# A hybrid encoder layer on one core: another order of the projection jobs, and linear-attention levels with one instruction per step for both directions

## The chip, the cores and the metric

The kernel runs on one core of one Trainium2 chip. The metric is the device time in microseconds (us) of one execution. Five engines are named as the profile names them: PE is TensorE (matmuls; PEld is its weight load), DVE is VectorE, ACT is ScalarE, POOL is GpSimd, and SP is the engine whose queue issues most of the transfers. Each engine works through its own queue in order and waits on semaphores for the others.

## What is computed

One layer is applied to two request groups with the same parameters: a prompt of 512 tokens and a sample of 1024 tokens, each 1024 wide. The input is normed and modulated, projected by one matrix of 1024 x 3360 whose columns go to four mixers and a gate, and projected back.

```python
def hybrid_layer(x, c, ...):
    shift, scale, gate = split(silu(c) @ ada_w + ada_b, 3)
    h = rms_norm(x, pre_g) * (1 + scale) + shift
    a_q, a_k, a_v, a_lr, b_u, c_q, c_k, c_v, d_u, d_v, z = split(h @ w_in)
    out_a = gla_branch(a_q, a_k, a_v, a_lr, ...)      # gated linear attention, both directions
    out_b = fnet_branch(b_u, fnet_w)                  # real part of a 2-D Fourier transform, then fnet_w
    out_c = attention_branch(c_q, c_k, c_v, ...)      # rms_norm and rotary on q and k; softmax; 8 heads, 2 for k and v
    out_d = sgu_branch(d_u, d_v, ...)                 # u * (w_s @ rms_norm(v) + b_s) in chunks of 128 tokens
    mixed = concat([out_a, out_b, out_c, out_d]) * silu(z)
    return x + gate * rms_norm(mixed @ w_out, post_g)

# gated linear attention of one direction, per head (4 heads, 32 wide in k, 64 in v):
#   a_r = sigmoid(lr_r @ w2 + b2) ** (1 / 16)
#   o_t = sum over s <= t of (q_t * prod(a_r, r = s+1..t)) . k_s  v_s
# the other direction runs over the flipped tokens, with s < t; both are added and normed
```

All inputs and outputs are float32.

## The kernel before

**Groups and jobs.** The 1536 tokens are worked in three groups of 512: group 2 is the prompt, groups 0 and 1 are the halves of the sample. For each group the projection is cut into jobs: A (queries, keys, values and the low-rank gates of linear attention, called GLA), dv and du of the gating mixer with its mix, b (Fourier), kv and q (attention), and z, the gate path, ten jobs of 128 columns. For float32 accuracy every operand is split into a rounded high part and a low part (oph and opl, the halves of a weight tile wt), and each product is three matmuls. A weight unit of 128 x 512 is loaded raw, cast on ACT (L306) and its low part subtracted on POOL (L98), or on DVE where the table LOW_V says so, which it does for job b of group 2; both halves are stored in DRAM (parts), and groups 0 and 1 load them from there (L298). gemm_tm (L314) makes 256 columns for 512 tokens: 8 blocks x 4 token blocks x 3 matmuls of 256 columns. gemm_fm (L337) makes 128 columns with the tokens on the free axis: 8 x 3 matmuls of 512 columns.

**What follows a job.** Nearly all results go to DRAM and come back later. z (L452): three exponential or logarithm passes on ACT (tile ze), one DVE product (zr), a store to zT from SP's queue (L464). q and kv (c_path, L490): an ACT copy (cev, kev), a square, a reduction, an inverse root in small steps, two DVE products, two POOL products (rp_t), one DVE sum, and the store to qd or kvd from SP's queue (L509, L501); this is called rope here (L391). dv and du: ACT copies into dvu; then the mix, twelve matmuls on normed dv and four DVE instructions that read them (L446).

**The main chain.** For group 2: GLA first pass, second pass, Fourier mixer (fnet), key preparation (kv_path), attention. Then GLA of group 0, fnet over groups 0 and 1, GLA of group 1, key preparation and the second GLA pass over both, and the sample's attention in eight stages (attend). The output projections of finished groups (out_first, out_last) run beside it.

**What sets the order.** The jobs are traced inside `later()` (L513), which lowers their priority, so that they fill TensorE beside the main chain. The framework plans the order of each queue when the program is built, from priorities and its own time line. A log, flog, counts the columns of the filler matmuls in thousands; after_columns (L93) queues a matmul behind the point where the log reaches a number. The order of the jobs before: for group 2 and 0, A, dv, du, b, mix, kv, q (jobs, L1220), then z with the input preparation of the next group hooked in before its jobs 6 and 9 (next_prep, L1234), then a part of the gate of the modulation (gate_path). Group 1 starts with b and has its z among the last fillers (L1296).

**GLA first pass (L762).** The two directions are worked as a binary tree with levels m = 1, 2, 4, ..., 64 over 512 tokens. At a level the keys of one half of each pair of m-blocks meet the queries of the other half: qsi and ksx serve one direction, qpi and kpx the other. Each level splits those halves into high and low parts (kh, kl, qh, ql), one instruction for each direction's half, runs 48 matmuls of 32 rows (L815) and puts the result into st under a mask (L820, four DVE copies). Then the queries and keys are multiplied by the products of the decay factors (ntf, ntb). After the levels, st is multiplied with the values (L866, L867, with its casts sth and stl), and the keys are transposed for the states. LEVEL_AT places the level m = 2 of a group, and each later level a step further, in the filler's column count:

```python
LEVEL_AT = {2: (124, 12), 0: (548, 13), 1: (806, 13)}
```

## Time and profile before

| | |
|---|---|
| median of 3 runs | 1240.02 us (1235.35 to 1246.15) |
| the profiled execution | 1240.43 us, span 1238.6 us |
| PE busy | 1105.1 us, 89% of the span |
| DVE, ACT, POOL busy | 61%, 48%, 31% |
| mean granted TensorE clock | 0.943 |
| DMA | 233.99 MB, mean 189 GB/s |

The profile is one execution on the chip. Its page gives busy times, a strip in 40 slices and groups of equal instructions: the line, engine and operation, the tiles as out<-in with shapes, the count, the busy time and the mean in ns, then the idle time of the engine ahead of them and what ended it. Other views group the same records by a stretch of time, by tile, by who waited for whom, or list them in order of time. A line number may be that of a helper, as L86 (all split matmuls), L98 (all subtractions), L101 (products) and L104 (sums).

### The profile page before, as it was taken

Reading aid. Unit: us, or ns where it says so; the run is one execution under the profiler, and the core shown is the slowest. Engines: PE = TensorE matmul, PEld = TensorE weight load, DVE = VectorE, ACT = ScalarE, POOL = GpSimd, SP = SyncE. Lnnn points to the kernel's source line nnn. Section 1 sums busy time; section 2 is a strip of 40 time slices with the busy share of each in tenths; the row PEclk is TensorE's granted clock in tenths of the full one; section 3 lists DMA queues with packets and bytes.
Section 4 is the critical chain, followed back from the end, with each engine's and each line's share of the span. In section 5 each row is a group of like instructions: output and inputs, shape, how many; then the busy total and the mean of one; then the engine's idle time right before and its main releaser. Section 6 shows DMA issues by size and latency. Waiting matters only on the chain. (4 is left out here: it accounts for less than half of the span.)

```text
span 1238.6 us, 21385 instructions
## 1 busy us (share of the span) xinstructions
PE 1105.1 (89%) x7906; PEld 973.3 (79%) x7906; DVE 754.5 (61%) x1440; ACT 597.3 (48%) x1472; POOL 382.0 (31%) x372
## 2 busy tenths in 40 slices
PE   5998779998999888998898899788989999988995
PEld 1587768764999886767898778588989998977995
DVE  6439776647454299552239852774787568686615
ACT  4334246643565235462123244444675667666623
POOL 3136654561011147113016510553141011223003
PEclk9999798998999998999999789789999999999998
DMA  8497656877433765576765346678347333264272
GB/s 316 159 324 243 227 183 202 309 271 234 150 117 116 239 198 159 173 251 199 250 203 168 112 147 194 197 252 282 128 145 247 111 103 94 81 212 130 82 252 97
DMA packets 126393, 233.99 MB, mean 189 GB/s; under 512 B 13092, under 2 KB 65796, under 8 KB 126288
## 3 DMA queue, kind: packets, MB, share of 16 engines
q1 hardware_dynamic: 121624, 227.49, 56.0%
q10 hardware_dynamic: 4664, 5.13, 1.2%
q8 instruction: 62, 1.02, 0.3%
q14 instruction: 43, 0.35, 0.1%
HBM read 162.97 MB, written 69.61 MB: 188 GB/s over the span
## 5 line engine op out<-in xcount | busy, mean ns | idle before, releaser
L86 PE MATMUL ps_mm<-wt,oph 128*128 128x256 f32 x2240 | 443.2, 293 | 20.7 <-DMA wt<-parts 11.0
L86 PEld LDWEIGHTS ps_mm<-wt,oph 128*128 128x128 f32 x2240 | 368.6, 199 | 30.6 <-DMA wt<-parts 11.3
L86 PE MATMUL ps_mm<-wt,opl 128*128 128x256 f32 x1120 | 326.0, 292 | 0.0
L86 PEld LDWEIGHTS ps_mm<-wt,opl 128*128 128x128 f32 x1120 | 222.0, 199 | 1.8
L86 PE MATMUL ps_mm<-oph,wt 128*128 128x512 f32 x576 | 194.8, 410 | 12.7 <-DMA wt<-parts 6.1
L554 DVE TENSOR_REDUCE nm<-ps_s 128x1 f32<-128x512 f32 x160 | 108.9, 686 | 58.6 <-PE ps_s L553 57.8
L86 PEld LDWEIGHTS ps_mm<-oph,wt 128*128 128x128 f32 x576 | 112.8, 197 | 38.9 <-ACT kh L797 3.8
L98 DVE TENSOR_TENSOR ptl<-ps_t,pth 128x512 fp32r<-128x512 f32 x160 | 108.4, 685 | 56.7 <-ACT pth L571 56.2
L98 POOL TENSOR_TENSOR wt<-wr,wt 128x512 fp32r<-128x512 f32 (+1 forms) x68 | 90.4, 1333 | 140.5 <-ACT wt L306 131.9
L571 ACT CAST pth<-ps_t 128x512 fp32r<-128x512 f32 x160 | 91.2, 590 | 65.8 <-PE ps_t L569 64.8
L561 ACT ACTIVATE pr<-ps_s,nm 128x512 f32<-128x512 f32 x160 | 109.5, 692 | 20.9 <-DVE nm L557 16.2
L86 PE MATMUL ps_mm<-opl,wt 128*128 128x512 f32 x288 | 117.9, 409 | 0.0
L569 PE MATMUL ps_t<-cs,pr 128*128 128x128 f32 x640 | 91.6, 276 | 1.1 <-DVE nm L557 0.6
L306 ACT CAST wt<-wr 128x512 fp32r<-128x512 f32 (+1 forms) x80 | 47.6, 597 | 77.5 <-PE ps_mm L86 36.0
L569 PEld LDWEIGHTS ps_t<-cs,pr 128*128 128x128 f32 x640 | 76.3, 143 | 9.5 <-PE ps_s L553 1.0
L101 POOL TENSOR_TENSOR oc<-oc,den 128x256 f32<-128x256 f32 x24 | 14.8, 629 | 220.3 <-DVE oc L104 199.0
L86 PEld LDWEIGHTS ps_mm<-opl,wt 128*128 128x128 f32 x288 | 56.7, 197 | 11.4
L552 PE MATMUL ps_s<-kT,qT 128*128 128x512 f32 x128 | 56.5, 442 | 5.0 <-ACT pr L561 4.8
L98 POOL TENSOR_TENSOR opl<-m,oph 128x512 fp32r<-128x512 f32 x30 | 39.1, 1319 | 52.6 <-ACT oph L1086 52.6
L553 PE MATMUL ps_s<-kT,qT 128*128 128x512 f32 x128 | 51.3, 401 | 0.0
L101 POOL TENSOR_TENSOR yt<-yt,gp 128x512 f32<-128x512 f32 x20 | 25.9, 1293 | 81.9 <-ACT jk L1118 64.8
L86 PE MATMUL ps_o<-pth,vkv 128*128 128x256 f32 x256 | 41.7, 285 | 0.6 <-DVE nm L557 0.6
(349 smaller groups left out, 2112.6 us busy)
## 6 DMA issues: line engine op xcount, KB each, us to landing
wt<-parts SPq DMA_DIRECT2D x136, 512.0 KB, 3.6
parts<-wt SPq DMA_DIRECT2D x68, 512.0 KB, 4.7
wr<-wp SPq DMA_DIRECT2D x48, 256.0 KB, 3.8
adar<-ada SPq DMA_DIRECT2D x16, 512.0 KB, 6.0
zT<-zr SPq DMA_DIRECT2D x30, 256.0 KB, 2.8
zt<-zT SPq DMA_DIRECT2D x30, 256.0 KB, 5.0
mt<-mixd SPq DMA_DIRECT2D x24, 256.0 KB, 5.2
wr<-wo SPq DMA_DIRECT2D x20, 256.0 KB, 4.5
```

The costliest lines, as they stand in the source:

```text
L86: t = T.matmul(out, a, b, start=first and i == 0, stop=last and i == len(terms) - 1, skip_group_check=skip)
L98: e.tensor_tensor(out, a, b, ALU.subtract)
L101: e.tensor_tensor(out, a, b, ALU.mult)
L306: (V.tensor_copy if part_engine(HIGH_V, u, S) is V else S.copy)(h, raw)
L552: T.matmul(sp, qT[:, h, qc], kT[kv][:, kc], start=True, stop=False)
L553: T.matmul(sp, qT[:, h, qc], kT[2 + kv][:, kc], start=False, stop=True)
L554: V.tensor_reduce(nm[:, f:f + 1], sp, AX, ALU.max, negate=True)
L561: S.activation(pr, sps[f], AF.Exp, bias=nm[:, 0:1], accum_out=rsum[:, b, h, f:f + 1])
L569: T.transpose(pt[:, k * 128:(k + 1) * 128], pr[f][:, k * 128:(k + 1) * 128], ident)
L571: S.copy(pth[f][:, :, qc], ptv)
```

## The change

**Order of the jobs.** z follows A at once, in all three groups. dv, du, b and the mix follow, and keys and queries come last (a new function `queries`). Group 1 ends its jobs with kv; its queries take the place that its z had among the last fillers. The input preparation of the next group is cut in two: in_prep_x builds the four diagonal blocks on DVE into one tile, and in_prep_b, behind the kv job, makes one matmul of 512 columns in place of four of 128.

**GLA.** The queries of both directions lie in one tile q2, the keys in k2, the factors in one tile ff of three rows. cross(t, m) is the view that takes the right half of each pair for both directions at once, so each split, each factor product and each level of decay products is one instruction where there were two. An ACT copy fills k2 with the keys twice, and one exponential more fills the third row of ff.

**Places.** LEVEL_AT is changed, and the first fold of fnet is queued behind the end of job b plus 14 thousand columns.

```diff
-HA = 6
-HB = 9
 HC = 3
 LEVELS = (1, 2, 4, 8, 16, 32, 64)
-LEVEL_AT = {2: (124, 12), 0: (548, 13), 1: (806, 13)}
+FOLD_AT = 14
+LEVEL_AT = {2: (131, 12), 0: (571, 12), 1: (829, 12)}
...
+        rsb = gm.tile([128, 512], F32, tag="rsb", bufs=1, name="rsb")
+        for b in range(4):
+            V.tensor_scalar(rsb[:, b * 128:(b + 1) * 128], ident, rs[:, b:b + 1], None, ALU.mult)
+        return rsb
+    def in_prep_b(rsb):
         pt = ps_mm()
-        for b in range(4):
-            dg = gm.tile([128, 512], F32, tag="h32", bufs=3, name="dg")[:, 0:128]
-            V.tensor_scalar(dg, ident, rs[:, b:b + 1], None, ALU.mult)
-            T.matmul(pt[:, b * 128:(b + 1) * 128], ones, dg, start=True, stop=True)
-        rsb = gm.tile([128, 512], F32, tag="rsb", bufs=1, name="rsb")
+        T.matmul(pt, ones, rsb, start=True, stop=True)
         V.tensor_copy(rsb, pt)
...
-    def zpath(g, hooks):
+    def zpath(g):
         job[0] = ("z", g)
         for j in range(10):
-            if j in hooks:
-                hooks[j]()
...
+    def c_kv(g):
...
+    def c_q(g, hook):
+        job[0] = ("c", g)
         for j in range(2):
+            if j:
+                hook()
...
+        ff = pool.tile([128, 3, 512], F32, tag="ff", bufs=1, name="ff")
...
+            f = ff[:, 1 - d, :]
             V.tensor_scalar(f, pl, bg[:, d:d + 1], 0.0, ALU.add, ALU.min)
             sub(G, f, f, t)
+            if d:
+                S.activation(ff[:, 2, :], f, AF.Exp, scale=1.0 / 16.0)
             S.activation(f, f, AF.Exp, scale=1.0 / 16.0)
-            ff.append(f)
...
-        qpi = ppool.tile([128, 512], F32, tag=f"qpi{g}", bufs=1, name=f"qpi{g}")
-        qsi = ppool.tile([128, 512], F32, tag=f"qsi{g}", bufs=1, name=f"qsi{g}")
-        ksx = pool.tile([128, 512], F32, tag="ksx", bufs=1, name="ksx")
-        mul(V, qpi, aq, ff[0])
-        mul(V, qsi, aq, ff[1])
-        prod = pool.tile([128, 512], F32, tag="kpx", bufs=1, name="prod2")
-        for i, src in enumerate((qsi, qpi)):
-            qv, kv, pv = (t.rearrange("p (n two) -> p two n", two=2) for t in (src, ak, prod))
-            mul(G, pv[:, i], qv[:, i], kv[:, 1 - i])
+        pad = 2 * 512 + 2 * LEVELS[-1]
+        q2 = ppool.tile([128, pad], F32, tag=f"q2{g}", bufs=1, name=f"q2{g}")
+        k2 = pool.tile([128, pad], F32, tag="k2", bufs=1, name="k2")
+        qsi, qpi, ksx, kpx = q2[:, 0:512], q2[:, 512:1024], k2[:, 0:512], k2[:, 512:1024]
+        def cross(t, m):
+            v = t[:, 0:2 * (512 + m)].rearrange("p (i c) -> p i c", i=2)[:, :, 0:512]
+            return v.rearrange("p i (n two m) -> p i n two m", two=2, m=m)[:, :, :, 0, :]
+        def pair(t, m):
+            return t.rearrange("p (n two m) -> p two n m", two=2, m=m)
+        mul(V, q2[:, 0:1024].rearrange("p (i c) -> p i c", i=2), aq.unsqueeze(1).to_broadcast([128, 2, 512]), ff[:, 0:2, :])
+        prod = pool.tile([128, 512], F32, tag="prod", bufs=1, name="prod2")
+        for i in range(2):
+            mul(G, pair(prod, 1)[:, i], cross(q2, 1)[:, i], pair(ak, 1)[:, 1 - i])
+        S.copy(k2[:, 0:1024].rearrange("p (i c) -> p i c", i=2), ak.unsqueeze(1).to_broadcast([128, 2, 512]))
...
-            for i, src in enumerate((ksx, kpx)):
-                s_, h_, l_ = halves(src, m)[i], halves(kh, m)[i], halves(kl, m)[i]
-                S.copy(h_, s_)
-                sub(G, l_, s_, h_)
+            S.copy(pair(kh, m), cross(k2, m))
+            sub(G, pair(kl, m), cross(k2, m), pair(kh, m))
             qh = pool.tile([128, 512], F32R, tag="qh", bufs=2, name="qh")
             ql = pool.tile([128, 512], F32R, tag="ql", bufs=2, name="ql")
-            for i, src in enumerate((qsi, qpi)):
-                s_, h_, l_ = halves(src, m)[i], halves(qh, m)[i], halves(ql, m)[i]
-                S.copy(h_, s_)
-                sub(V, l_, s_, h_)
+            S.copy(pair(qh, m), cross(q2, m))
+            sub(V, pair(ql, m), cross(q2, m), pair(qh, m))
...
-            tfv, tbv = (t.rearrange("p (n two) -> p n two", two=2) for t in (tf, tb))
-            def bc(t, i):
-                return t[:, :, i].unsqueeze(2).to_broadcast([128, n2, m])
-            q1, q2 = halves(qpi, m)
-            mul(G, q2, q2, bc(tfv, 0))
-            q1, q2 = halves(qsi, m)
-            mul(G, q1, q1, bc(tbv, 1))
-            if m == 1:
-                k1, k2 = halves(ak, 1)
-                mul(G, halves(ksx, 1)[0], k1, bc(tfv, 1))
-                V.tensor_copy(halves(ksx, 1)[1], k2)
-                V.tensor_copy(halves(kpx, 1)[0], k1)
-                mul(G, halves(kpx, 1)[1], k2, bc(tbv, 0))
-            else:
-                k1, k2 = halves(ksx, m)
-                mul(V, k1, k1, bc(tfv, 1))
-                k1, k2 = halves(kpx, m)
-                mul(V, k2, k2, bc(tbv, 0))
-            ntf = pool.tile([128, n2], F32, tag=f"tf{n2}", bufs=1, name="ntf")
-            ntb = pool.tile([128, n2], F32, tag=f"tb{n2}", bufs=1, name="ntb")
-            mul(V, ntf, tfv[:, :, 0], tfv[:, :, 1])
-            mul(V, ntb, tbv[:, :, 0], tbv[:, :, 1])
-            tf, tb, ntot = ntf, ntb, n2
+            def factor(base):
+                v = gt[:, base + 1:base + 2 * ntot - 1].rearrange("p (i c) -> p i c", i=2)[:, :, 0:ntot - 1:2]
+                return v.unsqueeze(3).to_broadcast([128, 2, n2, m])
+            mul(G, cross(q2, m), cross(q2, m), factor(0))
+            mul(V, cross(k2, m), cross(k2, m), factor(ntot))
+            ng = pool.tile([128, 3 * n2], F32, tag=f"ng{n2}", bufs=1, name="ng")
+            gv = gt.rearrange("p (d n two) -> p d n two", d=3, two=2)
+            mul(V, ng.rearrange("p (d n) -> p d n", d=3), gv[:, :, :, 0], gv[:, :, :, 1])
+            gt, ntot = ng, n2
...
-                mms(pr[:, 0:256], terms)
+                with after_columns(max(b_end[g] for g in gs) + FOLD_AT) if j == 0 else nullcontext():
+                    mms(pr[:, 0:256], terms)
...
+        zpath(g)
         mix = sgu(g)
         next(mix)
         if g != 1:
             b_path(g)
         next(mix, None)
-        c_path(g)
-    def next_prep(g, n):
-        rsb = []
-        zpath(g, {HA: lambda: rsb.append(in_prep_x(n)), HB: lambda: in_prep_t(n, rsb[0], range(2))})
-        in_prep_t(n, rsb[0], range(2, KD))
+    def queries(g, n):
+        rsb = in_prep_x(n)
+        c_kv(g)
+        in_prep_b(rsb)
+        c_q(g, lambda: in_prep_t(n, rsb, range(2)))
+        in_prep_t(n, rsb, range(2, KD))
         gate_path(n)
...
-            next_prep(2, 0)
+            queries(2, 0)
             jobs(0)
-            next_prep(0, 1)
+            queries(0, 1)
             jobs(1)
+            c_kv(1)
...
-        zpath(1, {HB: lambda: t[0].extend(out_ops(2, KORD[:2]))})
+        c_q(1, lambda: t[0].extend(out_ops(2, KORD[:2])))
```

More of the change, by code (lines that the diff above doesn't have):

```diff
@@ L205, in in_prep_x @@
         rs = rsqrt(ss, 4, 1024, V)
-        pt = ps_mm()
-        for b in range(4):
-            dg = gm.tile([128, 512], F32, tag="h32", bufs=3, name="dg")[:, 0:128]
-            V.tensor_scalar(dg, ident, rs[:, b:b + 1], None, ALU.mult)
-            T.matmul(pt[:, b * 128:(b + 1) * 128], ones, dg, start=True, stop=True)
-        rsb = gm.tile([128, 512], F32, tag="rsb", bufs=1, name="rsb")
+        rsb = gm.tile([128, 512], F32, tag="rsb", bufs=1, name="rsb")
[3 more added lines that the diff above has]
+    def in_prep_b(rsb):
+        pt = ps_mm()
+        T.matmul(pt, ones, rsb, start=True, stop=True)
         V.tensor_copy(rsb, pt)
-        return rsb
     def x_start(pool):
@@ L488, in kv_path, with c_rows @@
             V.tensor_copy(kT[i][:, cols], pt)
-    def c_path(g):
+    def c_rows(g, src, pair, c0):
+        return src[g][pair * 256:(pair + 1) * 256, c0:c0 + 256].rearrange("(b p) c -> p b c", p=128)
+    def c_kv(g):
         job[0] = ("c", g)
-        def rows(src, pair, c0):
-            return src[g][pair * 256:(pair + 1) * 256, c0:c0 + 256].rearrange("(b p) c -> p b c", p=128)
         def ev_kv(pair, p):
@@ L500, in ev_kv @@
             for i in range(2):
-                nc.sync.dma_start(out=rows(kvd, pair, 0)[:, :, i * 128:(i + 1) * 128], in_=t[:, i])
+                nc.sync.dma_start(out=c_rows(g, kvd, pair, 0)[:, :, i * 128:(i + 1) * 128], in_=t[:, i])
         gemm_tm(opT[g], wp, JOFF[J_KV], 256, ev_kv)
+    def c_q(g, hook):
+        job[0] = ("c", g)
         for j in range(2):
+            if j:
+                hook()
             def ev(pair, p, j=j):
@@ L508, in ev @@
                 rope(t.rearrange("p b (h d) -> p b h d", h=4), 2, 4, (4 if g == 1 else 0) + 2 * pair, 0, 1)
-                nc.sync.dma_start(out=rows(qd, pair, 256 * j), in_=t)
+                nc.sync.dma_start(out=c_rows(g, qd, pair, 256 * j), in_=t)
             gemm_tm(opT[g], wp, JOFF[J_Q + j], 256, ev)
@@ L726, in gla_in @@
         sub(V, lrT[32:64, :], lr[32:64, :], lrT[32:64, :])
-        ff = []
+        ff = pool.tile([128, 3, 512], F32, tag="ff", bufs=1, name="ff")
         for d in range(2):
@@ L734, in gla_in @@
             S.activation(t, t, AF.Ln, bias=1.0)
-            f = pool.tile([128, 512], F32, tag=f"f{d}", bufs=1, name=f"f{d}")
+            f = ff[:, 1 - d, :]
             V.tensor_scalar(f, pl, bg[:, d:d + 1], 0.0, ALU.add, ALU.min)
             sub(G, f, f, t)
+            if d:
+                S.activation(ff[:, 2, :], f, AF.Exp, scale=1.0 / 16.0)
             S.activation(f, f, AF.Exp, scale=1.0 / 16.0)
-            ff.append(f)
         vhl = pool.tile([128, 4, 4, 2, 64], F32R, tag="vhl", bufs=1, name="vhl")
@@ L750, in gla_in @@
             sub(V, vhl[:, b, :, 1, :], pv, vhl[:, b, :, 0, :])
-        prod = pool.tile([128, 512], F32, tag="ksx", bufs=1, name="prod")
+        prod = pool.tile([128, 512], F32, tag="prod", bufs=1, name="prod")
         mul(G, prod, aq, ak)
@@ L782, in gla_pass1 @@
         add(V, o4, o4, avx)
-        kpx = pool.tile([128, 512], F32, tag="kpx", bufs=1, name="kpx")
         st = pool.tile([128, 4, 4, 128], F32, tag="st", bufs=1, name="st")
         G.memset(st, 0.0)
-        tf, tb = ff
-        ntot = 512
-        def halves(t, m):
-            v = t.rearrange("p (n two m) -> p n two m", two=2, m=m)
-            return v[:, :, 0, :], v[:, :, 1, :]
+        gt, ntot = ff.rearrange("p d c -> p (d c)"), 512
         def level(li, m):
@@ L946, in gla_pass2 @@
                               in_=ap_all[:, 4 * gi:4 * gi + 4, :])
+    b_end = {}
     def b_path(g):
@@ L955, in b_path @@
         gemm_tm(opT[g], wp, JOFF[J_B], 256, ev)
+        b_end[g] = flog[-1][0]
     def fnet(pool, gs, prompt):
```

3 lines of the change are left out of this document (1 added, 2 removed).

## The prediction

> **What bounds the kernel now.** The totals of the page come first.
>
> ```profile
> span 1238.6 us, 21385 instructions
> PE 1105.1 (89%) x7906; PEld 973.3 (79%) x7906; DVE 754.5 (61%) x1440; ACT 597.3 (48%) x1472; POOL 382.0 (31%) x372
> ```
>
> TensorE (PE) is the bound; no other engine is near. The change removes almost no matmul work, so whatever it wins must come out of the 133.5 us in which PE is not busy (1238.6 - 1105.1), or out of the time that PE runs at a lowered clock. The chain that ended last names only the final stores, so it says nothing here; I read stretches instead. In the next view each row is one stretch: its length, busy time of PE, PEld, DVE, ACT and POOL, the granted clock, the DMA share and GB/s. I cut the span where the main chain changes stage: GLA of the prompt (group 2), its FNet, its attention, GLA of group 0, GLA of group 1, the second GLA pass with the key preparation, and two parts of the last attention.
>
> ```profile
> 95.00:200.00 105.00, 84.56 (x799) 80.41 (x798) 78.86 (x137) 43.27 (x104) 61.28 (x59) 0.85 0.63 210
> 200.00:300.00 100.00, 88.57 (x408) 65.83 (x407) 69.00 (x127) 57.15 (x134) 52.06 (x48) 0.96 0.81 274
> 300.00:440.00 140.00, 135.05 (x1024) 128.59 (x1023) 59.92 (x121) 64.20 (x161) 15.36 (x21) 0.98 0.52 162
> 440.00:530.00 90.00, 79.41 (x634) 66.40 (x633) 71.26 (x130) 43.53 (x97) 41.05 (x41) 0.94 0.53 170
> 645.00:735.00 90.00, 78.85 (x689) 71.83 (x688) 69.33 (x135) 29.41 (x76) 42.65 (x47) 0.85 0.46 145
> 735.00:830.00 95.00, 83.50 (x437) 70.88 (x437) 57.09 (x113) 46.65 (x115) 30.02 (x31) 0.87 0.65 204
> 830.00:1000.00 170.00, 161.19 (x1251) 153.13 (x1250) 109.90 (x210) 100.14 (x253) 43.03 (x40) 0.99 0.54 184
> 1000.00:1130.00 130.00, 116.77 (x868) 107.71 (x867) 98.17 (x187) 90.86 (x237) 32.88 (x31) 0.97 0.42 135
> ```
>
> Idle is length less PE busy; I add a clock loss of (1 - clock) x busy. The three GLA stretches give 20.4 idle and 12.7 clock, 10.6 and 4.8, 11.2 and 11.8. So one microsecond of idle costs 1.62, 1.45 and 2.06 us there in all, because the clock falls with it. The FNet stretch has 11.4 and 3.5 (factor 1.31), 735 to 830 has 11.5 and 10.9 (1.95). Now who made PE wait in the three GLA stretches (three answers of the same view; us in total, times, longest):
>
> ```profile
> PE ps_o L867 <- DVE stl L98: 4.6, 1, 4.6
> PE ps_mm L86 <- DVE dvu L446: 2.5, 1, 2.5
> PE ps_o L866 <- ACT sth L861: 2.3, 1, 2.3
> PE ps_mm L86 <- ACT bev L953: 1.8, 1, 1.8
> ...
> PE ps_mm L86 <- DMA wt<-parts: 4.2, 2, 3.8
> PE ps_s L815 <- POOL kl L98: 3.2, 1, 3.2
> ...
> PE ps_s L815 <- DVE st L820: 7.2, 5, 3.7
> PE ps_mm L86 <- ACT kev L498: 2.2, 1, 2.2
> ```
>
> The waits on stl, st, kl and kev stand where VectorE (DVE) and GpSimd (POOL) are filled by two things at once: the GLA pass and the rotary work (rope) of keys and queries. Even the weight wait is one of these. The waits of the SP queue and its issues around 455 us:
>
> ```profile
> SPq L509 <- DVE cev L104: 48.5, 9, 9.3
> SPq L464 <- DVE zr L101: 31.0, 14, 3.9
> ...
> 451.69 0.32 SPq L298 DMA_DIRECT2D wt<-parts  x1
> 460.01 0.37 SPq L509 DMA_DIRECT2D qd<-cev  x1
> 460.49 0.41 SPq L298 DMA_DIRECT2D wt<-parts  x1
> ```
>
> The store of a query tile stands in the queue until DVE has finished its rope, and the next weight load behind it goes out only at 460.49, 8.8 us after the one before; PE then lacks weights.
>
> **The move of the jobs.** I count filler in thousands of matmul columns (k), as the program's own log does: the start of A is 57k, a 256-wide job 24.6k (8 x 4 x 3 matmuls of 256), the gate path (z) 123k, the mix 3k. Before, the level positions 124 to 184k (group 2) fall on b, mix, kv and q; 548 to 613k (group 0) on z; 806 to 871k (group 1) on q and z. After, group 2 has z up to 180k, then dv, b, mix, kv, q; its levels at 131 to 191k meet z and dv. Group 0 has b, mix, kv, q from 552k, so its levels (571 to 631k) meet b, mix, kv and part of q, but its GLA preparation, the 40k before, meets du and b and no rope. Group 1 has z from 727 to 850k and dv, du to 899k, under the levels at 829 to 889k; kv and q come after. So at all three GLA starts the rope is gone. Its cost, and that of z, per instruction:
>
> ```profile
> L101 DVE TENSOR_TENSOR cev<-cev,rope 128x512 f32<-128x512 f32 x12 | 12.2, 1020 | 5.2 <-POOL rp_t L101 5.2
> L101 POOL TENSOR_TENSOR rp_t<-cev,rope 128x256 f32<-128x256 f32 x24 | 24.1, 1024 | 22.4 <-DVE cev L101 13.6 <-DVE rs_a L130 8.1 <-ACT qh L803 0.7
> L101 DVE TENSOR_TENSOR zr<-ps_mm,ze 128x512 f32<-128x512 f32 x30 | 20.6, 685 | 30.6 <-ACT ze L461 30.6
> L461 ACT ACTIVATE ze<-ze 128x512 f32<-128x512 f32 x30 | 18.9, 631 | 0.7
> L98 POOL TENSOR_TENSOR wt<-wr,wt 128x512 fp32r<-128x512 f32 x60 | 81.8, 1367 | 126.5 <-ACT wt L306 119.1 <-DMA xT<-xT 4.4 <-PE ps_mm L1198 3.0
> ```
>
> A query evacuation has three such DVE passes, 3 x 1.02 = 3.1 us, and 2 x 1.02 on POOL; four per group make 12.3 and 8.2, the keys with half the width 3 more on DVE. A group's z costs DVE 10 x 0.685 = 6.9 us and ScalarE (ACT) three passes of about 0.63 each, 19 us.
>
> What goes, stretch by stretch. *Group 2*: stl and sth (their casts queue behind rope) and the waits on dvu and bev (mix and b leave), 11.2 us of idle at most. Against it, b put its four low halves on DVE by a table; z puts them on POOL, 4 x 1.37 = 5.5 us more on an engine busy 58% there. I keep 6 of 11.2: 6 x 1.62 = 9.7 gained (ends 0 and 18). *Group 0*: the weight wait and kl, 7.4; I keep 5: 7.2 gained (ends 0 and 10.7), as the levels themselves still meet kv. *Group 1*: st and kev, 9.4; I keep 4.5: 9.3 gained (ends 0 and 19), since four PSUM copies per level stay on DVE whatever is beside them and the step falls from 13k to 12k.
>
> What comes. The ropes of group 2 go to where z stood, 200 to 300 us, beside the second GLA pass and FNet, with the mix and b ahead of them. DVE there: 69.0 - 6.9 + 15.3 = 77.4 of 100 us, the share that the group 0 stretch has now (71.3 of 90) with slightly more idle. The store of qd is now in SP's queue ahead of FNet's table loads and of the x loads of the next group. Between nothing and all 11.2 us of moved waits at 1.31 (14.7 us), I take 5. Group 1's queries move past the GLA levels into 735 to 830: DVE 57.1 + 12.3 less some z, about 66 of 95; 0 to 6, I take 2. The z of group 0 moves under the prompt's attention: ACT 64.2 + 19 less ten plain copies at about 0.6, 77 of 140, so its exponentials stay hidden, and 1 us covers it (0 to 3). z's stores at the first GLA start stand ahead of GLA's own loads in SP's queue, 3.9 us at the worst, but PE has filler then. The levels of group 1 end 18k later in the filler (889 for 871), so the last attention has 18k less to cover it. A column's time:
>
> ```profile
> 82.73 0.40 PE L86 MATMUL ps_mm<-wt,oph 128*128 128x256 f32 x2
> ...
> 83.09 0.52 PE L86 MATMUL ps_mm<-wt,oph 128*128 128x256 f32 x3
> ```
>
> Three matmuls of 256 take 0.36 us, so 18k take 8.4 us; if filler is one part in three of PE there, which I assume, they cover 25 us of attention. The stretch 1000 to 1130, where filler runs out, loses (13.2 + 3.5)/130 = 12.8%, the one before (8.8 + 1.6)/170 = 6.1%: 25 x 6.7% = 1.7 us.
>
> **The GLA levels.** Two 256-wide instructions become one 512-wide over the same elements. The rows of the halves, and a 512-wide ACT cast:
>
> ```profile
> L797 ACT CAST kh<-ksx 128x256 fp32r<-128x256 f32 x18 | 7.3, 408 | 43.6 <-PE ps_o L815 20.8 <-DVE ksx L101 15.9 <-POOL ksx L101 3.8
> L306 ACT CAST wt<-wr 128x512 fp32r<-128x512 f32 x72 | 44.5, 618 | 71.1 <-PE ps_mm L86 34.9 <-DMA parts<-wt 12.8 <-POOL vkvq L98 5.3
> L98 POOL TENSOR_TENSOR kl<-ksx,kh 128x256 fp32r<-128x256 f32 x18 | 15.0, 831 | 17.5 <-PE ps_o L815 12.5 <-ACT kh L797 4.9
> L101 POOL TENSOR_TENSOR qsi<-qsi,ntb 128x256 f32<-128x256 f32 x18 | 16.9, 938 | 20.0 <-DVE ql L98 20.0
> L101 DVE TENSOR_TENSOR ksx<-ksx,ntf 128x256 f32<-128x256 f32 x18 | 13.3, 738 | 0.0
> ```
>
> Per level ACT falls from 4 x 0.41 to 2 x 0.62 (0.4 us), POOL from about 2 x 0.83 + 2 x 0.94 = 3.5 to 2 x 1.37 (0.8 us). DVE's k product goes from 2 x 0.74 to one that I put at the 1.02 of the rope row, the nearest 512-wide one under the same crowding (0.5 us less; ends 0.69 and 2.1). All of it lies beside filler matmuls; it only helps the waits above come true, so it has no term of its own. The ACT broadcast copy of k, the second exponential, the diagonal of the input norm built on DVE with one matmul in place of four, and the later fold of FNet are a few microseconds on engines with slack, hidden by filler: nothing. If that cover were gone, they would cost about 3 us per group.
>
> Something speaks against the wide form: DVE and POOL hold each other up. Two places of the timeline (start, length in us):
>
> ```profile
> 144.59 0.75 POOL L101 TENSOR_TENSOR qsi<-qsi,ntb 128x256 f32<-128x256 f32 x1 [1.31 <-DVE ql L98]
> 144.76 0.85 DVE L101 TENSOR_TENSOR ksx<-ksx,ntf 128x256 f32<-128x256 f32 x1
> ...
> 486.25 1.43 POOL L101 TENSOR_TENSOR qsi<-qsi,ntb 128x256 f32<-128x256 f32 x1 [1.83 <-DVE ql L98]
> 486.43 0.41 DVE L101 TENSOR_TENSOR ksx<-ksx,ntf 128x256 f32<-128x256 f32 x1
> ```
>
> The same k product takes 0.85 us beside POOL's q product at the first place; at the second it takes 0.41 and POOL's takes 1.43 instead of 0.75. A 512-wide instruction makes the other wait longer. [...]
>
> Sum: -9.7 - 7.2 - 9.3 + 5 + 2 + 1 + 1.7 = -16.5. The profiled execution took 1240.43 us (span 1238.6 and 1.8 around it), 0.4 above the median of the three runs: 1240.4 - 16.5 = 1224.
>
> **Rivals.** *The wide instructions lock each other out; no change.* If each of a level's two DVE steps (k product, q low half) first waits out a whole 1.37 us POOL instruction, they take 2 x 2.06 = 4.1 us instead of the 2.4 of now, 1.7 us more. If half of it reaches PE at its fixed place in the order, 18 levels cost 15 us: 1239. For it: PE waits on L815 already. Against: there are half as many instructions to be blocked, and POOL's sum falls. Chance 0.20.
>
> *Slower.* The rope goes into the places where the second GLA pass, FNet and the key preparation run on DVE, and holds up SP's queue there as it did at 455. It decides if DVE is late by more than the three tiles of evacuation buffer cover. Then the waits of group 2 return in full (+14.7), 735 to 830 loses a weight wait like that of 4.2 us at 1.95 (+8), and POOL, with z's low halves at the first GLA start, eats group 2's gain; groups 0 and 1 keep half (-8.3), and the 1 and 1.7 stay: +17, 1257. For it: POOL is already busy 52 of 100 us in that stretch. Against: DVE's share above. Chance 0.14.
>
> *All waits go and little comes back*: most of 18 + 10.7 + 19, about -38: 1202. Chance 0.10.
>
> **The numbers.** The forecast, 1224, has the remaining 0.56 and a range of its own of 1208 to 1232. The measurement tells about 1% (12.4 us) from no change. Faster by more than that, under 1227.6: most of the forecast (0.47) and the large gain (0.10), 0.57; within 1%: 0.29; slower: 0.14. The range 1203 to 1250 leaves out a little of both outer rivals.
>
> **What would show it.** Right: DVE below its present share in the stretches of groups 0 and 1 up to the first level, no qd store ahead of a weight load there, the clock of the GLA stretches above 0.9 and their PE idle down by about 15 us together; slightly more idle in FNet and in the key preparation. Lock-out: L815 waiting on ql or kl at most levels, and k products near 2 us. Slower: stalls on weights or evacuation beside FNet. I am wrong altogether if the idle at the GLA starts comes from GLA's own serial steps and stays without the rope.

## The result and the profile after

The kernel before took 1240.88 us (median; 1235.35 to 1246.15), the changed kernel 1228.28 us (1223.29 to 1231.59). The ratio is 0.9895 with a 95% interval of 0.9865 to 0.9925: about 1% faster, 12.6 us, where 16.5 us were forecast. The profiled execution of the changed kernel took 1223.29 us. Its totals:

```profile
span 1221.5 us, 21183 instructions
PE 1091.1 (89%) x7894; PEld 957.8 (78%) x7894; DVE 738.4 (60%) x1374; ACT 597.8 (49%) x1442; POOL 370.8 (30%) x327
```

PE's idle time fell by only 3.1 us (133.5 to 1221.5 - 1091.1 = 130.4). Its busy time fell by 14.0, for nearly the same number of matmuls, so on average each held PE for less time. A net of 3 us of idle can hide large moves in both directions; the same stretches as in the prediction show them.

```profile
95.00:200.00 105.00, 93.72 (x777) 79.92 (x776) 68.23 (x95) 57.78 (x130) 58.74 (x42) 0.95 0.69 234
200.00:300.00 100.00, 81.93 (x545) 67.21 (x544) 77.54 (x157) 49.88 (x123) 52.98 (x52) 0.91 0.78 255
300.00:440.00 140.00, 138.57 (x870) 123.56 (x868) 53.46 (x102) 67.99 (x158) 9.92 (x13) 1.00 0.58 179
440.00:530.00 90.00, 74.48 (x744) 70.42 (x743) 61.06 (x111) 35.06 (x76) 36.65 (x29) 0.89 0.49 155
645.00:735.00 90.00, 87.12 (x801) 78.66 (x801) 54.28 (x101) 42.76 (x105) 29.44 (x21) 1.00 0.60 191
735.00:830.00 95.00, 71.55 (x493) 66.64 (x493) 74.90 (x144) 38.81 (x94) 52.39 (x51) 0.80 0.59 189
830.00:1000.00 170.00, 165.45 (x1281) 157.06 (x1281) 123.13 (x234) 110.78 (x281) 35.16 (x34) 0.99 0.48 157
1000.00:1130.00 130.00, 118.43 (x863) 110.82 (x862) 92.28 (x176) 82.96 (x216) 32.29 (x30) 0.93 0.44 139
```

Idle plus clock loss, worked out as in the prediction, in us. The windows are the same times in every kernel, so where a kernel runs ahead, a window holds slightly later work. Each column is one profiled execution. The last is the change with one mend, e3 below.

| stretch | before | after | change | forecast | e3 |
|---|---|---|---|---|---|
| 95 to 200, GLA of group 2 | 33.1 | 16.0 | -17.1 | -9.7 | 5.8 |
| 200 to 300, FNet | 15.0 | 25.4 | +10.4 | +5 | 16.5 |
| 300 to 440, prompt attention | 7.7 | 1.4 | -6.3 | +1 | 2.2 |
| 440 to 530, GLA of group 0 | 15.4 | 23.7 | +8.3 | -7.2 | 18.4 |
| 530 to 645, FNet of the sample | 12.4 | 8.8 | -3.6 | none | 8.1 |
| 645 to 735, GLA of group 1 | 23.0 | 2.9 | -20.1 | -9.3 | 8.0 |
| 735 to 830, key preparation, second pass | 22.4 | 37.8 | +15.4 | +2 | 41.7 |
| 830 to 1130, last attention | 27.2 | 26.1 | -1.1 | +1.7 | 18.6 |

Two GLA stretches gained about twice what was forecast, one lost, and 735 to 830 lost more than any stretch was said to. Who made PE wait now, at the places that lost (200 to 300, 440 to 530, 735 to 830):

```profile
PE ps_mm L213 <- DVE rsb L207: 10.9, 1, 10.9
...
PE ps_o L861 <- ACT sth L856: 7.0, 1, 7.0
PE ps_s L824 <- DVE st L829: 5.7, 1, 5.7
...
PE ps_mm L1082 <- DMA mt<-mixd: 9.1, 3, 5.8
PE ps_t L486 <- DVE kT L487: 4.2, 2, 2.1
```

The first line is the input norm of the next group, which the prediction had put at nothing. The timeline of the changed kernel gives its chain: SP's loads of x, the store of the mix, ACT's squares, DVE's diagonals, PE's matmul.

```profile
209.73 0.45 SPq L200 DMA_DIRECT2D xt<-x_s  x1
210.44 0.37 SPq L450 DMA_DIRECT2D mixd<-dvu  x1
220.32 0.38 SPq L200 DMA_DIRECT2D xt<-x_s  x1
...
227.97 1.05 ACT L203 ACTIVATE jk<-xt 128x1024 bf16<-128x1024 f32 x1
...
235.15 0.87 DVE L207 TENSOR_SCALAR rsb<-cs,rs_r 128x128 f32<-128x128 f32 x4
...
236.16 2.04 PE L213 MATMUL ps_mm<-rsb,ones 128*128 128x512 f32 x2 [10.88 <-DVE rsb L207]
```

The two x tiles are of the kind xy, of which there are two, and dvu and vhl of the mix hold both. The second load of x is issued 9.9 us after the store of the mix (210.44 to 220.32). Before, the gap was nearly as long (the mix stored at 137.46 us, the second load issued at 145.45), but kv, two query jobs and six of z lay between the mix and this matmul, 147k columns or some 69 us of PE (0.36 us for 768 columns, the prediction's row); now only the kv job does, 24.6k or some 12 us. At group 0 the same chain sits in ACT's queue ahead of the casts of a level:

```profile
474.46 1.06 ACT L203 ACTIVATE jk<-xt 128x1024 bf16<-128x1024 f32 x1 [3.66 <-DMA xt<-x_s]
...
476.89 0.60 ACT L808 CAST kh<-k 128x512 fp32r<-128x512 f32 x1
...
480.94 1.59 PE L824 MATMUL ps_s<-qh,kh 32*128 32x128 f32 x3 [5.67 <-DVE st L829]
```

ACT stands 3.66 us for a load of x with the cast kh behind it, and PE then stands 5.67 us ahead of that level's matmuls.

A new wait also stands in a stretch that gained. In GLA of group 2, z now evacuates beside the GLA start, and its product zr comes late on DVE:

```profile
118.07 7.24 DVE L100 TENSOR_TENSOR ng<-ng 128x384 f32<-128x384 f32 x6
...
127.06 0.68 DVE L100 TENSOR_TENSOR zr<-ps_mm,ze 128x512 f32<-128x512 f32 x1
...
127.79 0.79 PE L85 MATMUL ps_mm<-oph,wt 128*128 128x512 f32 x1 [6.66 <-DVE zr L100]
```

The six are the products of the decay factors, and they hold DVE for 7.24 us. PE stands 6.66 us for the zr behind them.

### The profile page after: what moved, and what is told of

It is laid out like the page before. It is cut to its first block, busy times and chain, and to the rows that moved or that the text cites. A ratio compares the mean times of both kernels' runs of the same rounds, so it can differ in the third digit from the quotient of the medians.

```text
span 1221.5 us, 21183 instructions
## 1 busy us (share of the span) xinstructions
PE 1091.1 (89%) x7894; PEld 957.8 (78%) x7894; DVE 738.4 (60%) x1374; ACT 597.8 (49%) x1442; POOL 370.8 (30%) x327
## 3 DMA queue, kind: packets, MB, share of 16 engines
q8 instruction: 62, 1.02, 0.3%
## 5 line engine op out<-in xcount | busy, mean ns | idle before, releaser
L85 PE MATMUL ps_mm<-wt,oph 128*128 128x256 f32 x2240 | 440.1, 292 | 11.2 <-DMA wt<-parts 5.2
L85 PEld LDWEIGHTS ps_mm<-wt,oph 128*128 128x128 f32 x2240 | 364.0, 196 | 22.9 <-DMA wt<-parts 7.1
L85 PE MATMUL ps_mm<-wt,opl 128*128 128x256 f32 x1120 | 321.8, 289 | 0.0
L85 PEld LDWEIGHTS ps_mm<-wt,opl 128*128 128x128 f32 x1120 | 218.8, 196 | 1.5
L85 PE MATMUL ps_mm<-oph,wt 128*128 128x512 f32 x576 | 190.8, 401 | 14.8 <-DVE zr L100 6.7
L85 PEld LDWEIGHTS ps_mm<-oph,wt 128*128 128x128 f32 x576 | 108.2, 190 | 42.6 <-DVE zr L100 6.8
L85 PE MATMUL ps_mm<-opl,wt 128*128 128x512 f32 x288 | 114.3, 397 | 0.0
L100 POOL TENSOR_TENSOR oc<-oc,den 128x256 f32<-128x256 f32 x24 | 14.9, 629 | 242.2 <-DVE oc L103 207.2
L100 POOL TENSOR_TENSOR yt<-yt,gp 128x512 f32<-128x512 f32 x20 | 26.1, 1308 | 79.9 <-ACT jk L1117 79.8
L100 DVE TENSOR_TENSOR zr<-ps_mm,ze 128x512 f32<-128x512 f32 x30 | 20.7, 689 | 47.9 <-ACT ze L460 47.7
```

The source lines that it names most:

```text
L85: t = T.matmul(out, a, b, start=first and i == 0, stop=last and i == len(terms) - 1, skip_group_check=skip)
L100: e.tensor_tensor(out, a, b, ALU.mult)
```

## The experiments

The theory was that the order is sound but for the input norm, that rope's move brings the gain, and that the wide instructions do nothing of their own. Each ratio is to the kernel before on the same chip.

**e1, the order alone.** The change with its job order and its LEVEL_AT, and gla_in, gla_pass1 and gla_pass2 of the kernel before.

```diff
-            S.copy(pair(kh, m), cross(k2, m))
-            sub(G, pair(kl, m), cross(k2, m), pair(kh, m))
+            for i, src in enumerate((ksx, kpx)):
+                s_, h_, l_ = halves(src, m)[i], halves(kh, m)[i], halves(kl, m)[i]
+                S.copy(h_, s_)
+                sub(G, l_, s_, h_)
...
```

> The changed kernel with the GLA passes of before: two instructions per step for the two directions, but the new job order, input preparation and level positions. The whole change took 12.6 us off the median (1240.88 to 1228.28). Theory that the order does it, since it takes the rope away from the GLA starts: this one keeps most of the gain, 1228 to 1233. Rival that the wide GLA instructions do it: this one is back near before, 1236 to 1242. If both are needed, because the level positions only fit a shorter level: slower than before, with PE waiting on level operands.

Measured: 1231.24 us (1229.58 to 1234.41), ratio 0.9922 (0.99 to 0.9945), as the first theory said. PE waits 11.7 us at L213 here too, so the wait for the input norm belongs to the order and not to the wide form.

**e2, the wide GLA alone.** The kernel before with those functions of the change, an edit the other way round.

```diff
-            for i, src in enumerate((ksx, kpx)):
...
+            S.copy(pair(kh, m), cross(k2, m))
+            sub(G, pair(kl, m), cross(k2, m), pair(kh, m))
...
-                mul(V, k1, k1, bc(tfv, 1))
-                k1, k2 = halves(kpx, m)
-                mul(V, k2, k2, bc(tbv, 0))
+            mul(V, cross(k2, m), cross(k2, m), factor(ntot))
...
```

> The kernel of before with the wide GLA instructions alone: old job order, old level positions. Theory that the order does the work: 1235 to 1241, since in the forecast the wide instructions had no term of their own. Rival that the wide instructions carry the gain: 1228 to 1232. The lock-out rival of the prediction would show here at its plainest, since rope still stands at the GLA starts: slower than before, k products near 2 us. In the changed kernel they took 0.785 us in the mean, so I expect no slowing.

Measured: 1226.47 us (1222.87 to 1229.26), ratio 0.9882 (0.9858 to 0.9905). This is faster than either range. By itself the wide form gains as much as the whole change, and the order (e1) nearly as much; together they do not add up, so neither alone is what carries the gain. Its stretch of group 1, whose row before had 78.85 busy at 0.85:

```profile
645.00:735.00 90.00, 84.38 (x723) 76.06 (x723) 67.81 (x124) 35.93 (x82) 36.25 (x30) 0.91 0.50 162
```

Idle plus clock loss falls from 23.0 to 13.2 us here, with the rope where it was; 300 to 440 falls by 5.1 and 530 to 645 by 2.7.

**e7, the wide form without its splits.** e2 with kh, kl, qh and ql of a level again in two instructions each.

```diff
-            S.copy(pair(kh, m), cross(k2, m))
-            sub(G, pair(kl, m), cross(k2, m), pair(kh, m))
+            for i in range(2):
+                S.copy(pair(kh, m)[:, i], cross(k2, m)[:, i])
+                sub(G, pair(kl, m)[:, i], cross(k2, m)[:, i], pair(kh, m)[:, i])
...
```

> The kernel before with the wide linear-attention code, except that the four splits of a level into high and low halves are again two instructions each; the products with the decay factors, the factor products and the start stay wide. It parts the 15 us that the wide code alone gained. Theory 'the gain is in what stands right before a level's matmuls, the splits on ScalarE, VectorE and GpSimd': most of the gain goes, 1236 to 1242, and waits of the level's matmuls on kl come back. Rival 'the gain is in the shorter stream of VectorE and GpSimd between two levels': most of it stays, 1226 to 1232.

Measured: 1235.3 us (1225.4 to 1239.0), ratio 0.9957 (0.9931 to 0.9982). This lies between the two ranges: some two thirds of e2's gain (0.75 of 1.18%, and by the two intervals the 0.75 can be 0.40 to 1.10) is in the splits, the steps right ahead of a level's matmuls, and the products keep the rest. The waits on kl did not come back. In 645 to 735 it is the waits on st (2.1 to 4.4 us) and qh (0.3 to 1.4) that grew against e2.

**e3, the input norm early.** The change, with in_prep_x traced behind z and ahead of dv, du and the mix.

```diff
         zpath(g)
+        rsb = in_prep_x(n) if n is not None else None
         mix = sgu(g)
...
     def queries(g, n, rsb):
-        rsb = in_prep_x(n)
```

> The changed kernel with the first half of the next group's input preparation (loads of x, squares, inverse root, diagonals) traced right behind the gate path instead of behind the mix, so that it no longer waits for the mix to give back its two tiles. In the changed kernel PE's longest wait is 10.9 us for the matmul of that preparation at 236 us, and ACT stands 3.7 us for a load of x at 474 us just ahead of a level whose masked copies then hold PE for 5.7 us. Theory that the delayed preparation is the cause: both waits go, 16.6 us of idle and some clock, 1205 to 1218. Rival that the planner's order only moves the same wait to another operand: 1224 to 1232.

Measured: 1206.22 us (1204.32 to 1211.75), ratio 0.9727 (0.9701 to 0.9753): 22 us less than the change. The waits on rsb at L213 and on st at L824 are gone, but not all of the gain is theirs. By the table FNet gives back 8.9 us and group 0 5.3; another 10.2 come from the stretch of group 2, where the order planned for DVE now has zr ahead of the last decay products and PE stands 1.05 us for it where it stood 6.66:

```profile
123.72 0.68 DVE L100 TENSOR_TENSOR zr<-ps_mm,ze 128x512 f32<-128x512 f32 x1
```

That shift was not aimed at. The loads of x now take the two tiles before the mix does, a whole group earlier:

```profile
21.36 0.94 SPq L200 DMA_DIRECT2D xt<-x_s  x2
206.01 0.44 SPq L200 DMA_DIRECT2D xt<-x_s  x1
216.52 0.38 SPq L200 DMA_DIRECT2D xt<-x_s  x1
```

These are group 0's at 21 us and group 1's at 206 and 217 us; in the change group 1's are issued at 462 and 469 us.

**e6, the same with the old GLA.** e1 with the edit of e3.

> The new order of the jobs with the early input preparation, but with the old linear-attention code (two instructions per step). The wide instructions alone gained 15 us on the kernel before, and only some 3 us on top of the new order, where other stalls stood in the way. Theory 'the two parts add up once the stall of the input preparation is gone': 1216 to 1225, that is 10 to 18 slower than the new order with early preparation and wide instructions (1206). Rival 'both parts remove the same waits (the levels beside the rope), so that one is enough': 1203 to 1212.

Measured: 1209.48 us (1207.55 to 1210.02), ratio 0.9753 (0.9733 to 0.9774). The interval overlaps that of e3, so the rival holds: once the norm is early, the wide form adds nothing that can be told from zero. 645 to 735 has 2.5 us of loss here without any wide instruction. Against e1 the gain is 22 us again, with 9.7 us of it in FNet and 10.1 at group 0.

**e5, no rope.** The kernel before without norm and rotation of queries and keys.

```diff
-            rope(t[:, 0].rearrange("p b (h d) -> p b h d", h=2), 2, 2, (4 if g == 1 else 0) + 2 * pair, 2, 3)
...
-                rope(t.rearrange("p b (h d) -> p b h d", h=4), 2, 4, (4 if g == 1 else 0) + 2 * pair, 0, 1)
```

> The kernel of before without the norm and the rotation of queries and keys (copy out of PSUM and store stay; attention then works on raw queries and keys, so the outputs differ). This is the most that moving the rope to a free place could give. Theory of the prediction: PE waits on stl, st, kl and on weights at the GLA starts go, 1215 to 1225. Rival that the GLA starts idle by their own serial steps: 1234 to 1240.

Measured: 1202.61 us (1200.47 to 1208.03), ratio 0.9696 (0.9666 to 0.9725). The rope costs some 38 us, more than was expected of it. The three GLA stretches lose 11.5, 8.8 and 13.0 us less than before, with every job in its old place. The waits on stl, sth and st and group 0's on kl and weights all but vanish there; kl, dvu and bev in group 2 (3.8, 2.5 and 1.7 us) and kev in group 1 (2.2) stay, so these are not the rope's.

**e8, the rope without its store.** The kernel before, with the rope of the queries on another tile, one of the three that z uses for zr, while the store still sends t and leaves out the rope. The keys are as before.

```diff
-                rope(t.rearrange("p b (h d) -> p b h d", h=4), 2, 4, (4 if g == 1 else 0) + 2 * pair, 0, 1)
+                ro = gm.tile([128, 2, 256], F32, tag="zr", bufs=3, name="ro")
+                rope(t.rearrange("p b (h d) -> p b h d", h=4), 2, 4, (4 if g == 1 else 0) + 2 * pair, 0, 1,
+                     ro.rearrange("p b (h d) -> p b h d", h=4))
```

> The kernel before, where the rope of the queries writes a tile of its own and the store sends the unrotated queries: the same work on every engine, but the store in SP's queue no longer waits for VectorE, and the evacuation buffer comes free earlier. The output is wrong in the queries' norm and rotation, which the store leaves out. Leaving the rope out altogether had given 38 us. Theory 'rope costs by its store, which holds the weight loads behind it in SP's queue': SP's waits on cev nearly vanish, the waits for weights fall from 17 to under 10 us, time 1212 to 1228. Rival 'it costs by the load that it puts on VectorE and GpSimd': 1234 to 1243, with the waits on st, stl and kl as before.

Measured: 1240.62 us (1235.97 to 1244.91), ratio 1.001 (0.9989 to 1.003). SP's waits on cev fall from 48.5 us, for DVE, to 13.8, for ACT's copy. PE's waits for weights fall from 17.1 to 11.3 us in all (under 10 was expected) and from 4.2 to 0.7 in 440 to 530, yet PE waits there all the same (waits of that stretch):

```profile
PE ps_s L819 <- ACT kh L801: 4.9, 1, 4.9
PE ps_s L819 <- POOL kl L98: 3.4, 1, 3.4
...
PE ps_mm L86 <- DMA wt<-parts: 0.7, 1, 0.7
```

The wait on kh was 0.2 us before. The weight wait was real, but with it gone PE waits for the level's casts instead. The prediction's reading of SP's queue named the wait that came last, not what the stretch costs. The edit does not free SP's queue altogether: one store of z now waits 13.6 us for a step of a root on DVE.

**Group 1, five placements**, all on e3. e9 moves its levels 17k columns earlier (812). e10 also puts its kv job ahead of dv, du and the mix, and e12 then the levels 17k further (795). e11 gives group 1 the order of before (A, dv, du, mix, kv, q, and z last; levels at 806 by 13). e13 has A, kv, q, dv, du, mix and z last (812 by 12).

```diff
-LEVEL_AT = {2: (131, 12), 0: (571, 12), 1: (829, 12)}
+LEVEL_AT = {2: (131, 12), 0: (571, 12), 1: (812, 12)}
...
         zpath(g)
+        if g == 1:
+            c_kv(g)
...
             jobs(1)
-            c_kv(1)
```

> The new order with early input preparation and wide instructions (1206), with the levels of group 1 queued 17 thousand columns earlier in the filler (812 for 829). After it, TensorE stood 14.5 us near 780 us for the second linear-attention pass to store its result, which the next filler (the output operands of group 0) reads. Theory 'the filler runs out because the levels of group 1 end too late': that wait falls by about 8 us (17 thousand columns), and with the clock that it costs the time falls to 1192 to 1202. Rival 'the levels then wait for their own chain or for dv and du': waits on st, kh or ql appear at 650 to 735 us, time 1204 to 1214.

> The new order with early input preparation, wide instructions and the levels of group 1 at 812 thousand columns (1202), with one more move: in group 1 the key and value job follows the gate path at once, and dv, du and the mix come after it. Placing the levels earlier alone left the second linear-attention pass where it was (its result stored at 779 and 791 us in both), so the levels were not what it waited for. Theory 'the key preparation, which is traced ahead of the second pass, waits for the key and value job, the last of group 1's jobs': with that job 49 thousand columns (some 23 us) earlier, the stores move to 765 to 780 us, the wait of TensorE for mixd falls from 15.5 us to under 6, time 1184 to 1196. Rival 'the second pass is bound by its own steps on VectorE and GpSimd': the stores move by less than 5 us and the time stays at 1198 to 1207.

> As the kernel with group 1's keys and values right behind its gate path, with the levels of group 1 at 795 thousand columns for 812. If the second pass waits for the levels once the key job is early, the time falls by another 2 to 6 us; if the levels then wait for their own chain (the gates and the decay products), waits on st, qh or ff appear at 640 to 730 us and it rises by 2 to 8 us.

> The new order with early input preparation and wide instructions (1206), with group 1 alone put back to the order of before: dv, du, mix, keys and queries, and its gate path among the last fillers, levels at 806 with steps of 13. Theory 'the 123 thousand columns of the gate path were the filler that covered the key preparation and the second pass, and the 49 thousand of the queries are too few': the idle time with its clock loss in 735 to 830 us falls from 41 to 22 to 28 us, and against it the levels of group 1 meet the rope again (645 to 735 us from 8 to 12 to 20): 1196 to 1207. Rival 'the filler there is not what is short': 735 to 830 us stays above 35 us, and the time rises to 1208 to 1218.

> The new order with early input preparation and wide instructions, with group 1 in a third order: keys and queries right behind A, then dv, du and the mix, and the gate path among the last fillers; its levels at 812 with steps of 12. Group 1 in the changed order (1206) lost its time at 735 to 830 us, group 1 in the order of before (1207) at the levels, 645 to 735 us; this order has no rope at the levels and 123 thousand columns of filler after them. Theory 'these two are separate losses and both go': 645 to 735 us at 4 to 9 us of idle time with clock loss, 735 to 830 us at 20 to 28, time 1188 to 1198. Rival 'the rope, wherever it is put, holds up VectorE for whatever stands there': the loss comes back in 530 to 645 us, beside the Fourier mixer of the sample, and the time stays at 1200 to 1210.

| | us | ratio (95%) | 645 to 735 | 735 to 830 |
|---|---|---|---|---|
| e3 | 1206.22 | 0.9727 (0.9701 to 0.9753) | 8.0 | 41.7 |
| e9 | 1202.18 | 0.9688 (0.9659 to 0.9718) | 1.5 | 40.7 |
| e10 | 1206.05 | 0.9726 (0.967 to 0.9782) | 6.0 | 37.9 |
| e12 | 1203.97 | 0.9717 (0.9665 to 0.9768) | 8.4 | 38.5 |
| e11 | 1206.84 | 0.9745 (0.9692 to 0.9799) | 14.9 | 26.0 |
| e13 | 1207.23 | 0.9737 (0.971 to 0.9764) | 13.7 | 28.1 |

All intervals overlap, those of e9 and e13 by less than 0.1%, and each kernel ran four to six times, so I call none of them faster. In the stretches, of one execution each, more can be told. With z last (e11, e13) 735 to 830 loses 13 us less than with the queries last, and 645 to 735 about 8 more (means of two and of four); within each kind the kernels differ by 4 and 7 us at most. e11's rows:

```profile
645.00:735.00 90.00, 79.91 (x674) 69.77 (x674) 54.83 (x107) 34.01 (x86) 26.11 (x24) 0.94 0.48 149
735.00:830.00 95.00, 77.55 (x491) 69.20 (x490) 59.85 (x115) 45.36 (x101) 46.86 (x44) 0.89 0.76 248
```

So e11's theory held in both stretches and in its time. e9's did not: 735 to 830 stayed as it was, and the 4 us in the median are not clear of noise; what went is loss in 645 to 735. e12's median is 2.1 us under e10's, within the noise, and the waits on st, qh and ff that its other outcome named do not appear at the levels.

In e10 the second pass was indeed released by the kv job: its results are stored at 763 and 777 us, in e3 at 779 and 791. But PE's wait did not shrink. In e10's timeline (SP's queue, then PE) it stands behind a store of queries:

```profile
774.51 0.37 SPq L515 DMA_DIRECT2D qd<-cev  x1
774.98 0.42 SPq L1073 DMA_DIRECT2D mt<-mixd  x1
...
778.26 1.09 PE L1082 MATMUL ps_mm<-cs,mt 128*128 128x128 f32 x4 [20.60 <-DMA mt<-mixd]
```

The load at 774.98 follows the two folded blocks of group 2, so by KORD it is that group's next block, long in DRAM; the expectation of e9, which took it for group 0's, had that wrong. In the view of SP's waits one query store alone waits 9.0 us for DVE, busy with ap_all of the second pass; in e3 the same load follows the store of the second pass, which waits 6.2 us for POOL. So at least 9.0 of the 20.6 us are queue order, and e10's theory held for the stores and fell for the time. In e13 both expected stretches missed (13.7 for 4 to 9, 28.1 for 20 to 28), and 530 to 645, at 9.8 against e3's 8.1, does not show the rival's return either. The order did not clear the levels as was meant: the last query tiles' rope still ran on DVE beside the first levels, where PE waits on ql and st:

```profile
664.45 1.59 DVE L103 TENSOR_TENSOR cev<-cev,rp_t 128x512 f32<-128x512 f32 x1
665.97 1.96 DVE L831 COPY_PREDICATED st<-mk,ps_s 128x512 f32<-128x512 uint8 x3
```

What bounds group 1 below 1202 stays open.

The best kernel run is e9, 1202.18 us, 37 us under the one before; its interval overlaps e3's.

## Why the prediction was right and wrong

**The total** held: 1224 forecast, 1228.28 measured. That it came so close is luck. The seven terms of the sum came to -10.5 us and not -16.5, with errors of 2.8 to 15.5 us in each that cancel, and 530 to 645, which had no term, gave 3.6 more. The gain of 12.6 us also lies right on the 12.4 at which the chances were parted.

**The signs** named were met in part. DVE's load at groups 0 and 1 fell (71.26 to 61.06 and 69.33 to 54.28 us), and the idle of the three stretches fell by 12.5 us where about 15 were said. The clock passed 0.9 at groups 2 and 1 (0.95 and 1.00) but not at group 0 (0.89). The idle of FNet and of 735 to 830 rose by 6.7 and 12.0 us, more than slightly.

**The gain at the GLA starts** was put at 9.7 + 7.2 + 9.3 = 26.2 us and was 17.1 - 8.3 + 20.1 = 28.9. Groups 2 and 1 came out near the upper ends given (18 and 19): the waits named there went nearly whole, and keeping about half of them was too careful. Group 2's list of 11.2 us left out the second longest wait of its stretch, 3.8 us on kl, which went too; and the 6.7 us on zr came in their place. That the rope beside the levels is a cause is shown by e5, and e1 and e6 show that the new order alone empties 645 to 735 (3.7 and 2.5 us). It is not the only one: mix and b left group 2's start as well, and kev, which the prediction put down to rope, stays in e5.

**Group 0** failed in sign. One step that failed is the one that costed the input norm at "nothing, hidden by filler". The edit was seen as a few instructions on engines with slack. What counted was where the chain stood: behind the tiles that the mix holds, with one job of 12 us to cover two loads, squares, a root and diagonals of some 26 us (209.73 to 236.16). It cost 10.9 us of PE's time in FNet and 5.7 at group 0. So the +5 for FNet was right only in its size's order: most of its 10.4 is this wait and not the moved rope, though DVE's load there was forecast well (77.4 us, measured 77.54). But the norm explains only 5.3 us at group 0: e3 still has 18.4 us there against 15.4 before. The 7.0 us on sth are in part the second half of the same input preparation, now between the query jobs: ACT's copies to st stand behind two oph steps that wait 3.15 and 2.80 us for DVE, and e3 keeps 4.5 of the 7.0. The rest of group 0's miss stays open.

**735 to 830** was put at +2, as rope on DVE, with DVE at about 66 us; it was at 74.90. Two things changed there together. The exchange of z for queries as the last filler takes 123k - 49k = 74k columns, at 0.36 us for 768 some 35 us of PE work, from the end of the filler; and it brings the queries' rope and its stores. In the stretch itself matmuls into ps_mm, most of them filler, held PE for 66.6 us before, 56.1 after and 61.1 in e11. PE's longest waits on DVE's tiles went from 6.3 to 11.4 us, those on mixd from 1.9 to 9.1. e11, with z last again, returns 15.7 us there and loses 6.9 at the levels, so the exchange is the cause; no run parts missing filler from added rope.

**The wide instructions** were given no term. Alone they gain 15.9 us (1242.39 to 1226.47), on the order with early norm nothing that can be told from zero (e6 to e3). "It only helps the waits above come true" fits the second case, not the first: at group 1 they are another way to remove the same waits.

**The lock-out** rival fell in its time and at the steps that it named. The rows after (18 levels):

```profile
L100 DVE TENSOR_TENSOR k<-k,ng 128x512 f32<-128x512 f32 x18 | 14.1, 785 | 0.3
L97 DVE TENSOR_TENSOR ql<-q,qh 128x512 fp32r<-128x512 f32 x18 | 13.9, 770 | 1.7 <-ACT qh L812 1.7
L100 POOL TENSOR_TENSOR q<-q,ng 128x512 f32<-128x512 f32 x18 | 27.6, 1533 | 28.0 <-DVE ql L97 28.0
L97 POOL TENSOR_TENSOR kl<-k,kh 128x512 fp32r<-128x512 f32 x18 | 26.1, 1448 | 17.7 <-ACT kh L808 17.3 <-PE ps_o L824 0.3
```

DVE's k product takes 0.785 us for both directions where one took 0.738, against the 1.02 taken and the 2.06 of the rival. POOL's two steps take 1.53 and 1.45, above the 1.37 of its weight subtraction. At 12 of the 18 levels k starts first, by 0.15 to 0.18 us, and POOL pays: its q product takes 1.43 to 1.49 us there, where its shortest takes 1.157:

```profile
139.12 0.67 DVE L100 TENSOR_TENSOR k<-k,ng 128x512 f32<-128x512 f32 x1
139.27 1.49 POOL L100 TENSOR_TENSOR q<-q,ng 128x512 f32<-128x512 f32 x1 [0.91 <-DVE ql L97]
```

DVE was held beside POOL elsewhere, at small instructions that the rival did not name. The decay products before (of one direction; the other's are alike in number) and after (count; shortest, median and longest in ns):

```profile
L101 DVE TENSOR_TENSOR ntf<-ntf x18: 153/172/949, 113.5 to 668.6; 128x128 f32<-128x128 f32 x3, 128x64 f32<-128x64 f32 x3, 128x32 f32<-128x32 f32 x3, 128x16 f32<-128x16 f32 x3
L100 DVE TENSOR_TENSOR ng<-ng x18: 165/1170/1449, 118.1 to 667.7; 128x384 f32<-128x384 f32 x3, 128x192 f32<-128x192 f32 x3, 128x96 f32<-128x96 f32 x3, 128x48 f32<-128x48 f32 x3
```

In the chain at 118.07 even the one of 128 x 12 takes 1.18 us (124.13 to 125.31); it starts when a q product of POOL has just ended (122.57 + 1.48 = 124.05) and the next POOL subtraction has begun (124.02). This is the chain that held zr, whose input ze was there at 121.15 us, and behind it PE for 6.66 us. In the pair above POOL's instruction is the one that takes longer (1.49 us for 1.157), in this chain DVE's (1.18 us, where the product of 128 x 12 at 667.75 us, with nothing on POOL beside it, takes 0.17). The rival had DVE wait every time. In the kernel before, too, a k product of DVE took longer beside a 512-wide step of POOL: 1.49 us (at 127.92) beside a weight subtraction, against 0.97 at most beside 256-wide products alone.

**The slower rival** had its place partly right (FNet and 735 to 830 lost 25.8 us together, near the 14.7 + 8 that it named), but in FNet the cause was the input norm and not rope on DVE, in 735 to 830 rope's share is not parted, and groups 2 and 1 gained far more than it allowed.

## What to carry to other kernels

When a chain is moved, cost the moment its first load can start, from who holds its tiles, and not the busy time of its instructions. When filler jobs change places, count the columns that each stretch of the main chain keeps beside it, and what their stores put ahead of loads in a queue. A wait that ends last names one of several things that are late: taking away its cause is worth little where the next one is due at the same time (e8), and two edits may each be worth nearly the whole gain and little more together (e1, e2). An instruction that looks too small to cost anything can be held for the length of a neighbour's (the decay product of 1.18 us, which takes 0.17 with POOL idle), and what stands behind it in its queue is late by the sum.

## What was unexpected of the hardware

A short wait of PE cost more afterwards than while it lasted. In the kernel before, the wait of 3.74 us on st ends at 683.72 us; slices of 3 us from there (same columns as the stretches):

```profile
681.00:684.00 3.00, 0.28 (x1) 0.27 (x1) 2.56 (x6) 1.02 (x3) 3.00 (x5) 0.96 0.05 14
684.00:687.00 3.00, 3.00 (x23) 2.36 (x26) 3.00 (x6) 0.00 (x0) 1.34 (x3) 0.50 0.70 207
687.00:690.00 3.00, 3.00 (x43) 2.88 (x40) 2.47 (x5) 1.43 (x4) 1.51 (x3) 0.50 0.17 46
690.00:693.00 3.00, 3.00 (x16) 3.00 (x16) 3.00 (x7) 0.00 (x0) 1.82 (x3) 0.50 0.42 117
693.00:696.00 3.00, 3.00 (x23) 3.00 (x23) 1.41 (x3) 2.09 (x5) 0.27 (x1) 0.84 0.15 60
696.00:699.00 3.00, 3.00 (x48) 2.87 (x46) 2.40 (x9) 1.04 (x4) 0.50 (x1) 1.00 0.55 175
```

The clock is at half for the next 9 to 10 us, though PE is busy throughout: 3 x 3 x 0.5 + 3 x 0.16 = 5.0 us lost on top of the 3.74, as an estimate by the prediction's clock loss. The matmuls show the clock: three of 256 columns take 0.36 us ahead of the wait (679.11 to 679.47) and 0.64 behind it (689.91 to 690.55). After the wait of 2.17 us that ends at 669.38 the half clock lasted 3.2 us, worked out from the loss in two slices (0.32 x 2.62 + 0.25 x 3 = 1.59 us, at half clock):

```profile
669.00:672.00 3.00, 2.62 (x15) 2.62 (x16) 2.97 (x8) 2.90 (x12) 2.05 (x3) 0.68 0.47 113
672.00:675.00 3.00, 3.00 (x21) 3.00 (x21) 3.00 (x5) 1.03 (x4) 2.54 (x3) 0.75 0.43 152
```

Why the two differ is not shown. The 32-row matmuls of a level run in the longer one up to 688.96 us, but the clock stays at half for five more, beside filler alone. Such losses of clock in the stretches from 95 to 1130 us add up to 54.7 us before and 45.6 after, which is 9 of the 14 us by which PE's busy time fell; the other 5 are not explained.
